# A two-layer hybrid mixer on one core: the convolution's taps held from before the stick heads until the choice of keys is done, their rest under the later early gates, and the convolution's norm behind the sparse heads

## The chip, the core and the metric

The kernel runs on one core of a Trainium2 chip. The metric is the device time of one execution in microseconds, as a median of several runs. The core has a matrix engine (TensorE, PE in the profile), a vector engine (DVE), a scalar engine (ACT), GpSimd (POOL), a queue engine that issues most transfers (SP) and 16 DMA engines. Each engine works through its own list of instructions in order; semaphores make one wait for another.

## What is computed

Two layers over 256 tokens of width 2048. Each layer normalises its input and projects it by one wide weight matrix; three token mixers work on the parts; their gated outputs are projected, merged by sigmoid gates, projected once more and added.

```python
h = rms_norm(x, norm_w)
proj = h @ w_in
(qa, ka, va, za, qi, ki, wi, ub, zb, qc, kc, vc, zc, gates) = jnp.split(proj, ...)
...
y_a = (dsa_attention(qa, ka, va, qi, ki, wi, top_k) * silu(za)) @ w_a_out
y_b = (conformer_conv(ub, conv_w, conv_b, cln_w, cln_b) * silu(zb)) @ w_b_out
y_c = (stick_breaking_attention(qc, kc, vc) * silu(zc)) @ w_c_out
g = sigmoid(gates).reshape(b, s, 3, D_MODEL)
merged = g[:, :, 0] * y_a + g[:, :, 1] * y_b + g[:, :, 2] * y_c
x = x + merged @ w_out
```

Branch A is a sparse attention: 16 small index heads (qi, ki, wi) score the keys, the 64 best of each query are chosen, and 8 heads attend to those alone. Branch B multiplies half of its projection by the sigmoid of the other, convolves each of 1024 channels over 31 past tokens, normalises over the channels and applies SiLU. Branch C is a stick-breaking attention of 8 heads: sigmoids of the products, running sums of logarithms over the keys, an exponential, and a product with the values.

## The kernel before

**Units and chunks.** All weights stream through PE in units of 512 KB. `load_unit` (L241) has SP issue the load into one of six `raw` buffers (L256); ACT rounds it to `wh` (`high`, L267), DVE subtracts to get the rest `wl` (`low`, L272); each has three buffers. PE multiplies both (all matmuls go through `mult`, L283). Eight units make a chunk of 512 columns (`chunk_W`, `chunk_N`); the chunk's sum stands in one of two `acc` tiles in PSUM, and a second pool of two tiles, `mm`, serves all smaller products. An `acc` tile is free again when its last reader is done, and the tile for a new chunk is given out by a scheduler that goes through the program as it will stand.

**Order of a layer.** After the convolution's input (`yT`) come, in this order on PE: the stick queries, keys and values (QC, KC, VC), the sparse queries QA (two chunks), index keys KI, values VA with the index weights, keys KA, index queries QI (eight chunks of 256), two early gates `early(1,0)` and `early(1,1)`, two more (`early(1,2)`, `early(1,3)`), then the branch gates ZC, ZB and ZA (two chunks each), the merging gates and the output projections.

**Work beside the units.** Three lists are advanced while the units run:
- `waiting` holds the convolution's taps. `taps` (L432) is four ACT activations (L441) and one DVE addition (L444) for four channel groups at one offset; 62 such taps per layer. `drain`, called by each `low`, runs at most one per unit, and none while `hold[0]` is set. `flush` runs all that is left at once.
- `turns` holds transpositions. `turn_in` (L171) copies an `acc` tile into two planes of 16 bits on ACT (L175), has SP issue two DMA transposes (L181) some units later, and joins the planes again (L189 on DVE, L191 on ACT or DVE).
- `stages` holds generators that yield after a number of units; `background` advances at most one turn or one of the first two stages per unit. `finish` runs them all to their end.

The generators that matter here: `stick` (L719) computes two stick heads: products, Abs/Exp/Ln on ACT, a split in two (L396, L397), the running sums as triangular products (L749 to L754), the difference (DVE L755), the exponential (ACT L756) and the mask (DVE L758), and the product with the values (L763, L765), copied by L767. `index_near` and `index_far` compute the index scores and choose the keys. `attend` (L907) computes four sparse heads for 128 queries: products (L915), softmax with exponentials on ACT (L924), transposes by DMA with ACT copies before and after (L933, L946), a split in two (L396, L397) and the product with the values (L953), copied by L955. `conv_norm` (L958) takes the means over channels by products with ones (L974), normalises, and applies SiLU. It needs all taps.

`early` (L898) multiplies one chunk of the merging gates ahead of its time, applies the sigmoid on ACT (L903, which needs another activation table than the copies) into a temporary of the pool `t4` (eight buffers, shared by taps, sticks and heads), and stores it by POOL (L904). `gate` (L408) multiplies a gate chunk, turns it with `turn_in` and applies SiLU.

**Where taps run before.** `hold[0]` goes up after QA's chunks (L786) and down after QI (L835). Before QA's end nearly all taps have run, one per unit; three entries are left for `flush()` (L957), which stands behind the first two early gates. `conv_norm` is started right there, then four `attend`, then `early(1,2)` and `early(1,3)`.

The instructions of each engine are written to a list by a scheduler that follows the order of the code, priorities (`high_priority`), `issue_after` and the buffers of the pools; so one moved call can move instructions of other calls.

Of the kernel before, what the change touches and what calls it, by code (L numbers as in the profile page):

```python
# [17 lines left out]
NT = S // P  # L18
# [38 lines left out]
def trunk(ctx: ExitStack, tc: tile.TileContext, x, xt, w_in, w_a, w_b, w_c, w_out,  # L57
# [38 lines left out]
    def nm(s):  # L96
        uid[0] += 1
        return f"{s}_{uid[0]}"
# [10 lines left out]
    def parts(n, own=()):  # L109
        own = list(own)  # L110
        return own + [slot(F32R).rearrange("p (k w) t -> p k w t", w=2) for _ in range(n // 4 - len(own))]
# [19 lines left out]
    def t4(dt=F32):  # L131
        return tp.tile([P, 1024], dt, tag="t4", bufs=8, name=nm("t4"))
# [7 lines left out]
    waiting = []  # L140
# [3 lines left out]
    def advance(e):  # L144
        try:
            e[1] = count[0] + next(e[0])
        except StopIteration:
            (stages if e in stages else turns).remove(e)
# [10 lines left out]
    def settle():  # L159
        while turns:  # L160
            advance(turns[0])
# [38 lines left out]
    def start(gen):  # L200
        stages.append([gen, 0])

    def finish():
        while stages:
            advance(stages[0])

    hold = [False]
# [12 lines left out]
    def flush():  # L220
        while waiting:
            for f in waiting.pop(0)[1]:
                f()
# [193 lines left out]
    def gate(c0, o, b, w, hx, park=None, slots=True, turn=TURN):  # L417
        def gated(k, z, v):
            nc.scalar.activation(v, z, AF.Silu)
            nc.vector.tensor_mul(z, v, o[:, k:k + 4, :])  # L420
            b.extend(parts(4))
            split_at(b, k, 4, z)
            if park is not None:
                for i in range(k, k + 4, 2):
                    nc.gpsimd.dma_start(park[:, i:i + 2], part(b, slice(0, 2), i, 2))

        for k in range(0, KC, 4):
            turn_in(chunk_W(w, c0 + k * P, hx), None, partial(gated, k), slots, turn)
# [60 lines left out]
    for layer in range(DEPTH):  # L489
# [277 lines left out]
            nc.scalar.copy(qcT[:, h0:h0 + 2, :], po[:, :512].rearrange("p (h t) -> p h t", h=2))  # L767

        settle()
        for h0 in range(0, NH, 2):  # L770
            start(stick(h0, STICK[h0 // 4]))

# [10 lines left out]

        for h in range(0, NH, 4):
            turn_in(chunk_W(w, O_QA + h * P, hx), qaT[:, h:h + 4, :], partial(spin, qaT[:, h:h + 4, :]))
        hold[0] = True  # L786
        kaT = t4()[:, :2 * S].rearrange("p (c t) -> p c t", c=2)
        ki = tp.tile([P, 2 * S], F32R, tag="ki", bufs=1, name=nm("ki")).rearrange("p (i c t) -> p i c t", i=2, c=1)
        rope(chunk_T(w, O_KI, P, hx, KD), None, partial(split, ki[:, 0], ki[:, 1]))
# [42 lines left out]
                turns.append([rotate(h - 2, v4), count[0]])  # L832
                advance(turns[-1])
        settle()
        hold[0] = False  # L835
        bias = {}

        def chosen(sc, bs, cb):
# [59 lines left out]
        def early(b, j):  # L898
            a = chunk_N(w, [(O_G + b * D + j * 512, 512)], hx, KD)
            sg_ = t4().rearrange("p (t d) -> p t d", t=NT)  # L900
            with tc.high_priority():
                for t in range(NT):
                    nc.scalar.activation(sg_[:, t, :], a[t], AF.Sigmoid)  # L903
            nc.gpsimd.dma_start(gates[b][:, :, j * 512:(j + 1) * 512].rearrange("t p d -> p t d"), sg_)  # L904
# [5 lines left out]
        def attend(t, c, qaT=qaT, kaT=kaT, va=va, bias=bias):  # L910
            n = (t + 1) * P
            ts_ = slice(t * P, (t + 1) * P)
            ps = mm_tile()
            for q in range(4):
                nc.tensor.matmul(ps[:, q * n:(q + 1) * n], qaT[:, c * 4 + q, ts_], kaT[:, c, :n],  # L915
                                 start=True, stop=True)
            lg = t4()
            l3 = lg[:, :4 * n].rearrange("p (h s) -> p h s", h=4)
            nc.vector.scalar_tensor_tensor(l3, ps[:, :4 * n].rearrange("p (h s) -> p h s", h=4), SCALE,
                                           heads(bias[t][:, :n], 4), op0=ALU.mult, op1=ALU.add)  # L920
            mx, sm = small(4), small(4)
            nc.vector.tensor_reduce(mx, l3, op=ALU.max, axis=AX.X, negate=True)
            for q in range(4):
                nc.scalar.activation(l3[:, q, :], l3[:, q, :], AF.Exp, bias=mx[:, q:q + 1],  # L924
                                     accum_out=sm[:, q:q + 1])
            nc.vector.reciprocal(sm, sm)
            nc.vector.tensor_mul(l3, l3, sm.unsqueeze(2).to_broadcast([P, 4, n]))
            own, cols = words(False)
            rows = own.rearrange("p (s w q k) -> p s w q k", s=NT, w=2, q=4)
            s16 = l3.bitcast(U16).rearrange("p q (s k w) -> p s q k w", k=P, w=2)  # L930
            for s in range(t + 1):
                for i in range(2):
                    nc.scalar.copy(rows[:, s, i], s16[:, s, :, :, i])  # L933
            yield 4
            for s in range(t + 1):
                    nc.sync.dma_start(cols.rearrange("p (g t) -> p g t", g=8)[:, :, s * P:(s + 1) * P],
                                      own[:, s * 1024:(s + 1) * 1024], transpose=True)
            yield 5
            c16 = cols.rearrange("p (w q s k) -> p w s q k", w=2, q=4, s=NT)
            into = own.bitcast(F32)[:, :4 * n]  # L940
            d16 = into.bitcast(U16).rearrange("p (s q k w) -> p s q k w", q=4, k=P, w=2)
            for s in range(t + 1):
                with tc.issue_after(lows[0].ins):
                    nc.vector.tensor_copy(d16[:, s, :, :, 1], c16[:, 1, s])
                with tc.issue_after(highs[0].ins):
                    nc.scalar.copy(d16[:, s, :, :, 0], c16[:, 0, s])  # L946
            ph, pl = pair(1024)
            split(ph[:, :4 * n], pl[:, :4 * n], into)
            yield 3
            po = mm_tile()  # L950
            for s in range(t + 1):
                for i, (u, v) in enumerate(((va[0], ph), (va[0], pl), (va[1], ph))):
                    nc.tensor.matmul(po[:, :512], u[:, s, c * P:(c + 1) * P], v[:, s * 512:(s + 1) * 512],  # L953
                                     start=s == 0 and i == 0, stop=s == t and i == 2)
            nc.scalar.copy(qaT[:, c * 4:c * 4 + 4, ts_], po[:, :512].rearrange("p (h t) -> p h t", h=4))  # L955

        flush()  # L957
        def conv_norm(cv=cv, pr=pr):  # L958
            work = t4()
            ph_ = pair(512)[0]  # L960

            def fold(w_, first, second):
                w4 = w_.rearrange("p (c t) -> p c t", c=4)
                nc.vector.tensor_add(w4, first, second)
                nc.vector.tensor_add(w_[:, :512], w_[:, :512], w_[:, 512:])
                nc.vector.tensor_add(w_[:, :S], w_[:, :S], w_[:, S:2 * S])
                h, l = ph_[:, :S], ph_[:, S:2 * S]
                nc.scalar.activation(h, w_[:, :S], AF.Copy, scale=1.0 / CW)
                nc.vector.scalar_tensor_tensor(l, w_[:, :S], 1.0 / CW, h.bitcast(F32), op0=ALU.mult, op1=ALU.subtract)

            def means():
                ps = mm_tile()
                for i in range(2):
                    nc.tensor.matmul(ps[:, :S], ones_r, ph_[:, i * S:(i + 1) * S], start=i == 0, stop=i == 1)  # L974
                return ps

            fold(work, cv[:, :4, :], cv[:, 4:, :])
            yield 3
            ps = means()
            sq = [t4().rearrange("p (c t) -> p c t", c=4) for _ in range(2)]  # L980
            for i in range(2):
                cs = cv[:, i * 4:i * 4 + 4, :]
                nc.vector.tensor_sub(cs, cs, heads(ps[:, :S], 4))
                nc.scalar.activation(sq[i], cs, AF.Square)
            fold(work, *sq)
            yield 6
            vs = means()
            r = rsqrt_mean(vs[:, :S], 1, t4())
            for i in range(2):
                cs = cv[:, i * 4:i * 4 + 4, :]  # L990
                nc.vector.tensor_mul(cs, cs, heads(r, 4))
                for c in range(4):
                    cc = i * 4 + c
                    lw, lb = pr[:, P_LW + cc:P_LW + cc + 1], pr[:, P_LB + cc:P_LB + cc + 1]
                    nc.scalar.activation(cs[:, c, :], cs[:, c, :], AF.Silu, bias=lb, scale=lw)
        start(conv_norm())
        for t in range(NT):
            for c in range(2):
                start(attend(t, c))


        for j in range(2, 4):
            early(1, j)
        gate(O_ZC, qcT, [], w, hx, parked[2], turn=OWN)
        gb = []
        gate(O_ZB, cv, gb, w, hx, slots=False, turn=LATE)
        finish()
        fast = FAST
        mix = [slot(F32R).rearrange("p a b -> p (a b)").rearrange("p (k i t) -> p k i t", k=KC, i=2)
# [304 lines left out]
```

## Time and profile before

| | us |
|---|---|
| median of 3 runs | 2026.02 (2025.62 to 2026.08) |
| the profiled execution | 2025.73 |
| its span, first to last instruction | 2024.0 |
| mean granted clock of PE | 0.997 of full speed |
| PE idle at L763, waiting for DVE L758 (2 times) | 4.1 |
| PE idle at L749, waiting for DVE L397 (2 times) | 1.8 |

The page of the profile gives busy time per engine and the groups of instructions. A row of the timeline has the start, the length, the engine, the line, the operation with its output and inputs, and, in brackets, how long the engine had been idle and who ended it. Consecutive instructions of one kind are one row with their number behind x. Where PE waits is also listed by line and cause. The granted clock is what the throttle left of full speed. Line numbers in the profile are those of the kernel before.

### The profile page before, as it was taken

What the parts mean: (1) busy time and instruction counts of PE and PEld (TensorE: products, weight loads), DVE (VectorE), ACT (ScalarE), POOL (GpSimd) and SP (SyncE); (2) the same over time, 40 slices, a digit from 0 to 9 for tenths busy, and PEclk for the clock granted to TensorE, in tenths of its full rate; (3) what the DMA queues carried; (4) which work ended last, traced back from release to release, by engine and by line L of the source; (5) the groups of instructions that cost most, each with busy time, mean ns of one, the idle gap of its engine ahead of it and who ended that gap; (6) DMA issues with size and microseconds to landing.
All of it is one profiled execution on the core that took longest, in us unless ns stands there. A gap on an engine that the chain in (4) does not pass through costs nothing. (4 is left out here: it accounts for less than half of the span.)

```text
span 2024.0 us, 26716 instructions
## 1 busy us (share of the span) xinstructions
PE 2006.2 (99%) x9566; PEld 1698.9 (84%) x9566; DVE 1560.7 (77%) x1708; ACT 1399.7 (69%) x1966; POOL 98.5 (5%) x156
## 2 busy tenths in 40 slices
PE   9999999999999999999999999999999999999998
PEld 7888889988888888888888888899888888888887
DVE  8688887797578888866676888878866888788665
ACT  7899696658776555556658997966587765555653
POOL 0000000000000100110000000000000012002100
PEclk9999999999999999999999999999999999999999
DMA  8788666766888877889867776666678999768983
GB/s 280 216 225 214 184 170 182 220 192 195 233 250 267 267 246 235 263 268 262 259 203 213 218 212 190 168 183 202 203 206 213 262 267 294 222 230 269 268 284 126
DMA packets 340278, 458.60 MB, mean 227 GB/s; under 512 B 109104, under 2 KB 159024, under 8 KB 340016
## 3 DMA queue, kind: packets, MB, share of 16 engines
q1 hardware_dynamic: 327040, 420.82, 71.2%
q0 software_dynamic: 11648, 33.56, 5.0%
q10 hardware_dynamic: 1456, 2.51, 0.4%
q8 instruction: 75, 1.23, 0.2%
q14 instruction: 59, 0.48, 0.1%
HBM read 413.30 MB, written 20.97 MB: 215 GB/s over the span
## 5 line engine op out<-in xcount | busy, mean ns | idle before, releaser
L283 PE MATMUL acc<-wh,s 128*128 128x512 f32 (+2 forms) x4736 | 1154.6, 386 | 1.5 <-ACT wh L267 1.5
L272 DVE TENSOR_TENSOR wl<-raw,wh 128x1024 fp32r<-128x1024 f32 (+1 forms) x714 | 858.6, 1207 | 316.1 <-ACT wh L267 312.3
L283 PEld LDWEIGHTS acc<-wh,s 128*128 128x128 f32 x4736 | 875.2, 188 | 178.7 <-ACT wh L267 2.8
L267 ACT CAST wh<-raw 128x1024 fp32r<-128x1024 f32 (+1 forms) x713 | 739.3, 1040 | 401.0 <-PE acc L283 323.7
L283 PE MATMUL acc<-wl,s 128*128 128x512 f32 (+2 forms) x2368 | 622.7, 385 | 0.2 <-DVE wl L272 0.2
L283 PEld LDWEIGHTS acc<-wl,s 128*128 128x128 f32 x2368 | 439.4, 188 | 89.7 <-DVE wl L272 0.6
L441 ACT ACTIVATE t<-s,cst 128x255 f32<-128x255 f32 (+14 forms) x480 | 199.1, 489 | 0.1
L444 DVE TENSOR_TENSOR s<-s,t 128x1020 f32<-128x1020 f32 (+14 forms) x120 | 138.6, 1155 | 1.5 <-ACT t L441 1.1
L283 PE MATMUL acc<-s,wh 128*128 128x384 f32 (+1 forms) x608 | 128.5, 353 | 0.0
L283 PE MATMUL mm<-wh,s 128*128 128x512 f32 x448 | 119.7, 389 | 0.0
L283 PEld LDWEIGHTS acc<-s,wh 128*128 128x128 f32 x608 | 106.3, 192 | 3.1
L283 PEld LDWEIGHTS mm<-wh,s 128*128 128x128 f32 x448 | 84.1, 188 | 17.5
L267 ACT CAST wh<-s 128x1024 fp32r<-128x1024 f32 x32 | 33.6, 1050 | 68.2 <-DVE s L1108 57.7
L283 PEld LDWEIGHTS acc<-s,wl 128*128 128x128 f32 x608 | 79.4, 191 | 1.0
L283 PE MATMUL acc<-s,wl 128*128 128x192 f32 (+1 forms) x608 | 79.8, 273 | 0.0
L234 POOL COPY sm<-sm 128x3 f32<-128x3 f32 x64 | 48.6, 759 | 502.1 <-ACT sm L233 502.1
L283 PE MATMUL mm<-wl,s 128*128 128x512 f32 x224 | 69.1, 390 | 0.0
L267 ACT CAST wh<-t 128x1024 fp32r<-128x1024 f32 x32 | 33.6, 1050 | 38.5 <-DVE t L1108 26.5
L904 POOL DMA_DIRECT2D gates<-t x8 | 6.0, 744 | 1108.1 <-ACT t L903 1058.9
L272 DVE TENSOR_TENSOR wl<-s,wh 128x1024 fp32r<-128x1024 f32 x32 | 39.2, 1225 | 26.0 <-ACT wh L267 25.8
L283 PEld LDWEIGHTS mm<-wl,s 128*128 128x128 f32 x224 | 41.9, 188 | 9.0 <-DVE wl L272 0.4
L272 DVE TENSOR_TENSOR wl<-t,wh 128x1024 fp32r<-128x1024 f32 x32 | 39.1, 1222 | 10.2 <-ACT wh L267 7.5
(241 smaller groups left out, 1277.1 us busy)
## 6 DMA issues: line engine op xcount, KB each, us to landing
raw<-in_w_in_dram SPq DMA_DIRECT2D x570, 512.0 KB, 4.4
raw<-in_w_out_dram SPq DMA_DIRECT2D x64, 512.0 KB, 5.3
raw<-in_w_b_dram SPq DMA_DIRECT2D x32, 512.0 KB, 5.0
raw<-in_w_c_dram SPq DMA_DIRECT2D x32, 512.0 KB, 4.9
raw<-in_w_a_dram SPq DMA_DIRECT2D x32, 512.0 KB, 5.5
parked<-s POOLq DMA_DIRECT2D x16, 512.0 KB, 5.8
t<-gates POOLq DMA_DIRECT2D x16, 512.0 KB, 6.5
s<-parked POOLq DMA_DIRECT2D x32, 256.0 KB, 5.6
```

Of the source, the lines that this page charges most:

```text
L234: seen = nc.gpsimd.tensor_copy(copy[:, :3], mark)
L267: highs[0] = nc.scalar.copy(u[1], u[0])
L272: sub = nc.vector.tensor_sub(u[2], u[0], u[1].bitcast(F32))
L283: newest[0] = nc.tensor.matmul(o, lhsT, rhs, start=start, stop=stop, skip_group_check=True)
L441: nc.scalar.activation(o[:, i, :S - d], yT[:, c, :S - d], AF.Copy, scale=wq)
L444: nc.vector.tensor_add(to, to, o[:, :, :S - d])
L904: nc.gpsimd.dma_start(gates[b][:, :, j * 512:(j + 1) * 512].rearrange("t p d -> p t d"), sg_)
```

## The change

`hold[0]` is set before the four stick generators are started, not after QA's chunks, and it is cleared after the first two early gates and the choice of keys (`finish()`), not after QI. The four `attend` are started before `early(1,2)` and `early(1,3)`, as these are written, and `conv_norm` behind both. `conv_norm` first yields, one unit at a time, until no tap is waiting. The call of `flush()` moves from ahead of it to behind the gates ZC and ZB.

In the order of the ACT engine, in layer 0, 17 taps move: 14 from units under QA and the sticks and 3 from the `flush`. They now stand one per unit in 17 units, from `early(1,2)` on into ZC.

The lines of the file shift: L903 becomes L902, L915 L914, L924 L923, L933 L932, L953 L952, L955 L954, L974 L982; those up to L767 move by one at most.

```diff
@@ -767,6 +767,7 @@
         settle()
+        hold[0] = True
         for h0 in range(0, NH, 2):
             start(stick(h0, STICK[h0 // 4]))
@@ -783,7 +784,6 @@
             turn_in(chunk_W(w, O_QA + h * P, hx), qaT[:, h:h + 4, :], partial(spin, qaT[:, h:h + 4, :]))
-        hold[0] = True
@@ -832,7 +832,6 @@
         settle()
-        hold[0] = False
         bias = {}
@@ -954,8 +953,17 @@
-        flush()
+        hold[0] = False
+        for t in range(NT):
+            for c in range(2):
+                start(attend(t, c))
+
+
+        for j in range(2, 4):
+            early(1, j)
         def conv_norm(cv=cv, pr=pr):
+            while waiting:
+                yield 1
             work = t4()
             ph_ = pair(512)[0]
@@ -994,16 +1002,10 @@
         start(conv_norm())
-        for t in range(NT):
-            for c in range(2):
-                start(attend(t, c))
-
-
-        for j in range(2, 4):
-            early(1, j)
         gate(O_ZC, qcT, [], w, hx, parked[2], turn=OWN)
         gb = []
         gate(O_ZB, cv, gb, w, hx, slots=False, turn=LATE)
+        flush()
         finish()
```

On PE, in the stretch of `early(1,3)` and the beginning of ZC, the value products of the heads stood between the units of ZC before (acc_772: ZC's first chunk, acc_801: its second):

```order
L283 MATMUL acc_772_4579<-wh_797_4715,s8_11_102 128x512 x8
L283 MATMUL acc_772_4579<-wl_798_4716,s8_11_102 128x512 x4
L953 MATMUL mm_799_4732<-ph_788_4674,t4_428_2534 128x512
L953 MATMUL mm_799_4732<-pl_789_4675,t4_428_2534 128x512
L953 MATMUL mm_799_4732<-ph_788_4674,t4_428_2534 128x512
L283 MATMUL acc_801_4740<-wh_803_4742,s8_8_99 128x512 x8
```

On PE after, the first of them stand inside the units (acc_719: `early(1,3)`, acc_770: ZC's first chunk):

```order
L283 MATMUL acc_719_4295<-wh_760_4503,s8_11_102 128x512 x6
L952 MATMUL mm_743_4422<-ph_728_4346,t4_414_2450 128x512
L283 MATMUL acc_719_4295<-wh_760_4503,s8_11_102 128x512 x2
L283 MATMUL acc_719_4295<-wl_761_4504,s8_11_102 128x512 x3
L952 MATMUL mm_748_4451<-ph_733_4370,t4_414_2450 128x512
```

The numbers in a name tell one tile from another. What moved: products of the heads' probabilities with the values now stand in the middle of a unit.

## The prediction

> **What bounds the kernel now.** I read the page's head first, then the waits of PE from 100 us on, then the timelines of PE, ACT, DVE and SP around each wait.
>
> ```profile
> span 2024.0 us, 26716 instructions
> PE 2006.2 (99%) x9566; PEld 1698.9 (84%) x9566; DVE 1560.7 (77%) x1708; ACT 1399.7 (69%) x1966; POOL 98.5 (5%) x156
> ```
>
> The profiled execution took 2025.73 us, 1.73 more than its span and 0.29 less than the median of 2026.02. PE, which multiplies the weight units, has work for 99% of the span. Time can be won only where PE stands still or runs at a lower clock, and anything that makes PE wait costs its full length. The waits of PE after the start are few:
>
> ```profile
> PE mm L763 <- DVE t L758: 4.1, 2, 2.1
> PE mm L749 <- DVE pl L397: 1.8, 2, 0.9
> PE acc L283 <- ACT wh L267: 0.4, 2, 0.3
> PE acc L283 <- DVE wl L272: 0.2, 1, 0.2
> ```
>
> The columns are total us, how often, and the longest one. Each of the first three comes once per layer, all at the stick heads (the generators `stick`, L719 to L767). In layer 0, on PE:
>
> ```profile
> 266.40 1.98 PE L283 MATMUL acc<-wh,s 128*128 128x512 f32 x8
> 269.12 1.98 PE L283 MATMUL acc<-wh,s 128*128 128x512 f32 x8
> ...
> 296.26 1.28 PE L283 MATMUL acc<-wh,s 128*128 128x272 f32 x8 [0.18 <-ACT wh L267]
> 297.38 0.66 PE L283 MATMUL acc<-wl,s 128*128 128x272 f32 x4
> 297.95 0.49 PE L749 MATMUL mm<-ph,upper_r 128*128 128x512 f32 x1
> 299.34 0.51 PE L749 MATMUL mm<-pl,upper_r 128*128 128x512 f32 x1 [0.90 <-DVE pl L397]
> ...
> 318.15 0.67 PE L763 MATMUL mm<-t,s 128*128 128x256 f32 x2 [2.03 <-DVE t L758]
> ```
>
> One full unit is 269.12 - 266.40 = 2.72 us of PE. The last unit of VA comes late by the cast (0.18 idle before it), then comes 0.90 behind L397, then 2.03 behind L758. And the last of these is followed by a lower granted clock. The columns of the windows are length, busy time of PE, PEld, DVE, ACT and POOL, granted clock, DMA share and GB/s:
>
> ```profile
> 299.00:304.00 5.00, 4.66 (x26) 4.10 (x27) 5.00 (x7) 4.94 (x7) 0.00 (x0) 1.00 0.95 302
> 318.00:323.00 5.00, 4.85 (x21) 4.65 (x22) 4.96 (x9) 2.89 (x6) 0.00 (x0) 0.66 0.37 108
> 323.00:330.00 7.00, 7.00 (x52) 7.00 (x51) 4.22 (x5) 3.65 (x5) 0.00 (x0) 1.00 0.48 128
> 1321.00:1326.00 5.00, 4.71 (x20) 4.58 (x21) 4.96 (x9) 2.96 (x6) 0.00 (x0) 0.66 0.37 108
> ```
>
> A clock of 0.66 over 5 us is (1 - 0.66) x 5 = 1.7 us of work not done, in both layers, each time behind the gap of two microseconds at L763. Behind the 0.90 at L749 there is none. So per layer the sticks cost about 0.2 + 0.9 at VA's end, and 2.0 + 1.7 at L763: 4.8 us, 9.6 in all. That is all that the first half of the change could win.
>
> **Part 1: the taps leave the sticks.** `hold` now goes up before the sticks start, so 17 taps per layer (14 in units under QA's chunks, 3 that `flush` put behind the gates) leave that stretch. What ACT does from the end of QA's last chunk on:
>
> ```profile
> 274.56 0.62 PE L283 MATMUL acc<-s,wh 128*128 128x512 f32 x2
> ```
> ```profile
> 274.81 1.91 ACT L175 COPY s<-acc 128x1024 uint16<-128x1024 uint16 x2
> 276.60 0.66 ACT L267 CAST wh<-raw 128x544 fp32r<-128x544 f32 x1
> 277.15 2.39 ACT L441 ACTIVATE t<-s,cst 128x230 f32<-128x230 f32 x6
> 279.43 0.58 ACT L767 COPY s<-mm 128x512 f32<-128x512 f32 x1
> 279.89 1.39 ACT L191 COPY s<-s 128x1024 uint16<-128x1024 uint16 x1
> 281.12 0.66 ACT L267 CAST wh<-raw 128x544 fp32r<-128x544 f32 x1
> 282.24 1.38 ACT L191 COPY s<-s 128x1024 uint16<-128x1024 uint16 x1 [0.46 <-DMA s<-s]
> ...
> 304.97 1.05 ACT L267 CAST wh<-raw 128x1024 fp32r<-128x1024 f32 x1 [0.98 <-PE acc L283]
> ```
> ```profile
> 276.74 3.41 SPq L181 DMA_TRANSPOSE s<-s  x2
> ```
>
> Taps run here as late as 277.15 to 279.43. But ACT then waits 0.46 for the transposes at 282.24, so it has caught up by then. Those transposes are issued by SP from 276.74, behind L175, whose start follows PE's end of the chunk at 274.56. None of this depends on the taps, so the second L191 starts at about 282.24 with them or without. After it ACT has no idle time until the 0.98 at 304.97, so the work up to VA's end is a chain from that L191 on. What the order changes there is one cast.
>
> On ACT, at the start of VA's units, before (wh_448 is the cast of a VA unit; the L191 rows are the two turns of QA's chunks):
>
> ```order
> L441 ACTIVATE t4_413_2441<-s8_80_536,cst_75 128x229 x4
> L767 COPY s8_137_854<-mm_421_2489 128x512
> L191 COPY s8_336_2021<-s8_379_2247 128x1024
> L267 CAST wh_448_2614<-raw_447_2613 128x544
> L191 COPY s8_336_2021<-s8_414_2461 128x1024
> L308 COPY ev_426_2523<-acc_417_2466 128x256
> ```
>
> On ACT, the same place after the change (wh_434 is that cast):
>
> ```order
> L191 COPY s8_336_2021<-s8_372_2205 128x1024
> L767 COPY s8_137_854<-mm_407_2405 128x512
> L191 COPY s8_336_2021<-s8_400_2377 128x1024
> L267 CAST wh_434_2530<-raw_433_2529 128x544
> L308 COPY ev_412_2439<-acc_403_2382 128x256
> ```
>
> The cast that filled ACT's wait for the transposes stands behind the second L191 now. It takes 277.15 - 276.60 = 0.55 us of ACT, and that much is added to the chain: +0.55 per layer at VA's end. The wait at L763 hangs on a chain that starts at KA's end, where ACT waits for PE once more:
>
> ```profile
> 312.56 0.59 ACT L308 COPY ev<-acc 128x512 f32<-128x512 f32 x1 [0.60 <-PE acc L283]
> ```
>
> So that wait stays, with its clock loss. Bounds for this part, per layer: -4.8 if all four losses go, -1.1 if only the two at VA's end go, +0.55 as worked out, and +0.55 + 1.7 if the gap at L749, then 1.45 us, starts a low-clock window too. I take +0.55, because the row at 282.24 shows a wait for DMA and not for taps.
>
> **Part 2: taps, attends and norm over the gates.** The 17 taps now run under `early(1,2)`, `early(1,3)` and the beginning of ZC. A tap is four activations:
>
> ```profile
> 261.97 1.05 ACT L267 CAST wh<-raw 128x1024 fp32r<-128x1024 f32 x1
> 262.93 1.63 ACT L441 ACTIVATE t<-s,cst 128x234 f32<-128x234 f32 x4
> 264.46 0.83 ACT L756 ACTIVATE t<-t 128x768 f32<-128x768 f32 x1
> ```
>
> A cast (0.96 to the next start) and a tap (1.53) are 2.49 of the 2.72 us of a unit, so the taps alone don't hold PE up; they leave ACT 0.23 us per unit for the heads' exponentials and copies, which have therefore moved later, onto ZC's units. Some products of `attend` (L915, L953; after: L914, L952) now stand inside units on PE, behind copies that ACT makes late. The order alone leaves them small margins. I take 0 for these, hidden by the three buffers of wh and wl; uncovered, one costs up to a late copy, about 1.05 us, at three such places per layer: 0 to +6.3 in all. Three taps leave `flush` and the norm moves behind the heads, towards ZB that uses it: 0, since the gates before it are 16 units or more long.
>
> **Part 3: the bank of ZC's second chunk.** A chunk accumulates in one of two `acc` tiles and frees it when ACT has copied it. The fourth early gate frees its tile with the sigmoids (L903, after: L902), ZC's first chunk with the pair at L175. On ACT before, at the end of ZC's first chunk (acc_729: the gate, acc_772: that chunk):
>
> ```order
> L903 ACTIVATE t4_771_4575<-acc_729_4356 128x512
> L267 CAST wh_797_4715<-raw_796_4714 128x1024
> L903 ACTIVATE t4_771_4575<-acc_729_4356 128x512
> L933 COPY t4_766_4550<-t4_763_4539 128x512 x2
> L267 CAST wh_803_4742<-raw_802_4741 128x1024
> L933 COPY t4_766_4550<-t4_763_4539 128x512
> L946 COPY t4_750_4471<-t4_751_4472 128x512
> L396 CAST ph_788_4674<-t4_750_4471 128x512
> L267 CAST wh_808_4768<-raw_807_4767 128x1024
> L946 COPY t4_766_4550<-t4_767_4551 128x512 x2
> L267 CAST wh_817_4808<-raw_816_4807 128x1024
> L175 COPY s8_800_4737<-acc_772_4579 128x2x512 x2
> ```
>
> On ACT after (acc_719: the gate, acc_770: ZC's first chunk):
>
> ```order
> L175 COPY s8_800_4727<-acc_770_4552 128x2x512 x2
> L932 COPY t4_767_4542<-t4_764_4531 128x512
> L902 ACT_TABLE_LOAD
> L902 ACTIVATE t4_769_4548<-acc_719_4295 128x512
> L267 CAST wh_815_4802<-raw_814_4801 128x1024
> L902 ACTIVATE t4_769_4548<-acc_719_4295 128x512
> ```
>
> On PE after, at the same boundary:
>
> ```order
> L283 MATMUL acc_770_4552<-wh_796_4702,s8_11_102 128x512 x8
> L283 MATMUL acc_770_4552<-wl_797_4703,s8_11_102 128x512 x4
> L283 MATMUL acc_801_4730<-wh_803_4732,s8_8_99 128x512 x8
> L283 MATMUL acc_801_4730<-wl_804_4733,s8_8_99 128x512 x4
> L283 MATMUL acc_801_4730<-wh_808_4758,s8_8_99 128x512 x8
> ```
>
> The sigmoids have moved from some ten rows ahead of the copies of ZC's first chunk to behind them: their t4 buffer comes free later, among the delayed taps and heads. So the tile that is free first for ZC's second chunk (acc_801) is that of ZC's first chunk itself: in the built program acc_801 lies in acc_770's banks (before, it alternated), and PE's first matmul of it waits for the second copy of L175, which can't start before PE has ended that very chunk. In the trace of before:
>
> ```profile
> 505.86 0.60 ACT L903 ACTIVATE t<-acc 128x512 f32<-128x512 f32 x1
> 507.29 0.60 ACT L903 ACTIVATE t<-acc 128x512 f32<-128x512 f32 x1
> ...
> 517.86 1.92 ACT L175 COPY s<-acc 128x1024 uint16<-128x1024 uint16 x2
> ```
>
> There the sigmoids end 10 us ahead of that boundary. The price: at QA's end the copies began 274.81 - 274.56 = 0.25 after PE's next start and took 1.91; a product starts about 0.05 behind its releaser, so PE stands for about 2.2 us, once per layer (bounds 1.9 to 2.5, by the start of L175 at the chunk's very end or behind a late cast). A gap of 2.03 was followed by 1.7 us of low clock in both layers, so I add that: 3.9 per layer. The Trainium skill ("TensorE: Matmul & The Clock Gate", section "What's actually happening") puts the half clock after at least one idle window of some 3.4 us; by it a gap of 2.2 us would cost only itself. The trace doesn't bear this out, since 2.03 us sufficed twice.
>
> **The sum.** 2025.73 + 2 x (0.55 + 2.2 + 1.7) = 2025.73 + 8.9 = 2034.6 as a profiled execution. With the 0.29 up to the median: 2034.9.
>
> **The rivals.**
> - *No low clock behind the new gap.* For it: the gap lies among full-clock units with a full supply of cast weights, and the gap of 0.90 had no such window. Against: 2.03 and its twin in layer 1. The Trainium skill's rule, above, is on this side. In both layers 2034.9 - 3.4 = 2031.5, in one 2033.2. Chance 0.17.
> - *More stalls*: the gap of 1.45 at L749 turns the clock down (+1.7 per layer), or the heads' products inside units wait for late copies (up to +3.1 per layer). For it: 0.23 us of ACT left per unit. Against: three buffers of slack. 2036.5 to 2041, chance 0.18.
> - *The sticks gain as well, beside the new gap.* Without taps all copies on ACT would start earlier than I think; this decides if the second L191 starts well ahead of 282.24. Against: that row waits for DMA. If the 1.1 at VA's end goes, 2034.9 - 2 x 1.65 = 2031.6; if all 4.8 go, the kernel is not slower: 2034.9 - 2 x (0.55 + 4.8) = 2024.2. Chance 0.04 each.
> - *Faster*: the sticks lose all their waits and PE finds acc_801's tile free. It needs L175 before the chunk's end, or another tile than the program shows: 2024.2 - 7.8 = 2016.4. Chance 0.03.
> - *Nothing reaches PE but the 0.55*: the bank wait is hidden, 2026.02 + 1.1 = 2027.1. Chance 0.04.
>
> **How the numbers follow.** The forecast itself has the remaining 0.50, with 2033.5 to 2036.5 as its own range by the bounds of the copies. 0.2% (4.05 us: 2021.97 and 2030.07) is about what a measurement of this kernel can tell from no change. Faster: 0.03. Same: 2024.2 and 2027.1, 0.04 + 0.04 = 0.08. Slower: the rest, 0.89. The range runs from 2031.0, just under the case without low clock, to 2040.0, which takes in most of the added stalls; outside lie the 0.11 of the three last cases and some 0.03 of the added stalls.
>
> **What would show it.** Right: in the waits of PE a new row, L283 behind ACT's L175, twice, about 2.2 each; a window of 0.66 or so behind it in each layer; L763 still 2.0 with its window; L749's wait 1.3 to 1.5 instead of 0.9; the sigmoids of the fourth early gate behind L175 in ACT's timeline. Wrong: no such wait, or no window behind it; L763's wait shorter; waits of PE at L914 or L952. If PE's busy time grows with no wait named, another cause lowered the clock.

## The result, and the profile after

The changed kernel takes 2040.49 us (median of 4 runs, 2038.46 to 2042.05), the kernel before 2026.05 (4 runs, 2025.62 to 2026.51): a ratio of 1.0071, with a 95% interval of 1.0053 to 1.0088. The direction was forecast, the size was not: 14.4 us instead of 8.9, half a microsecond above the range.

The profiled execution is the fastest of the four, at 2038.46 us, 12.7 more than the profiled one of before. The head of its page:

```profile
span 2036.7 us, 26721 instructions
PE 2009.9 (99%) x9566; PEld 1699.0 (83%) x9566; DVE 1561.5 (77%) x1708; ACT 1399.4 (69%) x1964; POOL 96.0 (5%) x156
```

DVE, ACT and PE's weight loads are as busy as before, within 1 us. PE is idle 9.0 us longer (26.8 instead of 17.8) and busy 3.7 us longer. The waits of PE from 100 us on (total us, times, longest):

```profile
PE acc L283 <- ACT s L175: 4.2, 2, 2.1
PE mm L763 <- DVE t L758: 4.1, 2, 2.1
PE mm L952 <- ACT ph L396: 3.0, 4, 1.1
PE acc L283 <- ACT wh L267: 1.8, 4, 0.7
PE mm L749 <- DVE pl L397: 1.8, 2, 0.9
PE acc L283 <- DVE wl L272: 1.5, 2, 1.0
```

The first row is the wait for the tile of ZC's second chunk, 2.1 once per layer; 2.2 was forecast. L763 and L749 stand as they stood; for L749 a wait of 1.3 to 1.5 was forecast, and it is 0.9. Against before there are two more new things: the heads' value products (L952) wait 3.0 in all, and the waits for casts at VA's end have grown from 0.4 to 1.8. On PE, around ZC's boundary and at the later heads:

```profile
515.09 1.07 PE L283 MATMUL acc<-wl,s 128*128 128x512 f32 x4
518.25 2.98 PE L283 MATMUL acc<-wh,s 128*128 128x512 f32 x8 [2.10 <-ACT s L175]
...
536.33 1.52 PE L283 MATMUL acc<-wh,s 128*128 128x512 f32 x6
538.27 0.51 PE L952 MATMUL mm<-ph,t 128*128 128x512 f32 x1 [0.41 <-ACT ph L396]
...
542.97 0.61 PE L283 MATMUL acc<-wl,s 128*128 128x512 f32 x2
544.66 0.50 PE L952 MATMUL mm<-ph,t 128*128 128x512 f32 x1 [1.08 <-ACT ph L396]
```

Four products of a wl take 0.91 (268.21 to 269.12 before, in the same kind of unit), so 518.25 - 515.09 - 0.91 = 2.25 us are lost at the boundary. At the heads, two wl products take 0.45: 544.66 - 542.97 - 0.45 = 1.24 lost; six wh products take 1.37: 538.27 - 536.33 - 1.37 = 0.57 lost. These waits come in the middle of a unit.

On ACT the copies that PE waits for at the boundary are

```profile
516.29 1.92 ACT L175 COPY s<-acc 128x1024 uint16<-128x1024 uint16 x2
```

and the sigmoids of the fourth early gate follow at 520.02 and 522.23, behind them, as forecast.

The chain of the third head group lost most of its time in SP's list, not on ACT. The copies and the first transposes of the third head group, in the changed kernel:

```profile
508.08 1.14 ACT L932 COPY t<-t 128x512 uint16<-128x512 uint16 x2
```
```profile
518.23 3.48 SPq L181 DMA_TRANSPOSE s<-s  x2
524.21 5.96 SPq L256 DMA_DIRECT2D raw<-in_w_in_dram  x3
530.26 3.33 SPq L935 DMA_TRANSPOSE t<-t  x2
```

The same in the run with the new order but early taps (below):

```profile
500.94 0.61 ACT L933 COPY t<-t 128x512 uint16<-128x512 uint16 x1
```
```profile
505.64 1.95 SPq L936 DMA_TRANSPOSE t<-t  x1
```

The copies end 7.7 us later (509.22 and 501.55), the first transpose is sent 24.6 us later. In the changed kernel it stands behind the transposes of ZC's first chunk (L181) and three more loads, and the profile shows no wait for data in front of it. So it is in all ten runs that have the new order: where the waits at the heads stay (the change in both its runs, sigmoids in ev, heads later, three repairs, ACT's half), the first transpose of this group goes out at 528 to 531, behind L181; where they go or shrink to 0.6 (taps left out, order alone, DVE's half, half the rate), at 505 to 513, ahead of it. Why the scheduler places it there isn't on record.

The windows of the clock, cut where the record of the granted clock changes (length, busy time of PE, PEld, DVE, ACT and POOL, granted clock, DMA share, GB/s). In the changed kernel, first around L763, then around ZC's boundary:

```profile
314.42:317.83 3.41, 2.65 (x19) 2.48 (x17) 3.38 (x6) 2.93 (x5) 0.00 (x0) 1.00 0.50 141
317.83:321.25 3.42, 2.12 (x13) 2.05 (x14) 3.08 (x6) 3.33 (x6) 0.00 (x0) 1.00 0.04 12
...
515.81:519.22 3.41, 1.31 (x6) 0.83 (x5) 1.95 (x2) 3.41 (x5) 0.00 (x0) 1.00 0.75 184
519.22:522.63 3.41, 3.41 (x9) 2.64 (x9) 0.00 (x0) 2.74 (x4) 0.00 (x0) 0.50 1.04 253
```

In the kernel before, around L763:

```profile
315.38:318.80 3.42, 1.39 (x11) 1.19 (x11) 3.04 (x6) 3.36 (x5) 0.00 (x0) 1.00 0.44 145
318.80:322.21 3.41, 3.41 (x14) 3.23 (x13) 3.41 (x6) 1.84 (x4) 0.00 (x0) 0.50 0.41 116
```

Half clock comes here for 3413 ns, after a stretch of the same length in which PE was busy for 1.3 or 1.4 us. The gap at L763 is as long after as before (2.06 and 2.03), but after, it falls across the edge of two stretches, which keep 2.65 and 2.12 us of work, and no half clock follows. The low-clock windows of this execution are therefore at ZC, as forecast, and no longer at L763, where the forecast had kept them.

The sum for the profiled execution, from start to start: ZC's boundary 2 x 2.25, the heads 2 x 1.8, VA's end about 1.3 in layer 0 (PE came to it 0.35 us earlier than before and left it 0.97 later) and 0.8 in layer 1 (below), one wait of 1.0 for L272 in the merging stage, and about 0.1 behind each of a dozen more switches between products and units. That is some 12 us. The low-clock windows are two in both executions and cancel.

The last unit of VA now starts with

```profile
297.23 1.27 PE L283 MATMUL acc<-wh,s 128*128 128x272 f32 x8 [0.66 <-ACT wh L267]
```

where it waited 0.18 at 296.26 before. Why that is 1 us later and not 0.55: on ACT after, at VA's start,

```profile
282.30 1.39 ACT L191 COPY s<-s 128x1024 uint16<-128x1024 uint16 x1 [3.22 <-DMA s<-s]
283.54 0.65 ACT L267 CAST wh<-raw 128x544 fp32r<-128x544 f32 x1
284.08 0.38 ACT L308 COPY ev<-acc 128x256 f32<-128x256 f32 x1
284.34 0.60 ACT L767 COPY s<-mm 128x512 f32<-128x512 f32 x1
285.31 0.40 ACT L408 COPY ev<-ev 64x256 f32<-64x256 f32 x1 [0.38 <-DVE ev L309]
```

and on DVE after:

```profile
284.22 0.73 DVE L272 TENSOR_TENSOR wl<-raw,wh 128x544 fp32r<-128x544 f32 x1 [1.13 <-ACT wh L267]
284.86 0.42 DVE L309 TENSOR_TENSOR ev<-acc,ev 128x256 f32<-128x256 f32 x1
```

ACT is idle for 3.22 us without the taps, and the second L191 still starts at 282.30, when the transposes land (282.24 before). The cast behind it costs its 0.55, and then its subtraction on DVE stands ahead of L309, for which ACT waits another 0.38.

### The profile page after: what moved, and what is told of

It reads as the page before. It is cut to its first block, busy times and chain, and to the rows that moved or that the text cites. A ratio compares the mean times of both kernels' runs of the same rounds, so it can differ in the third digit from the quotient of the medians.

```text
span 2036.7 us, 26721 instructions
## 1 busy us (share of the span) xinstructions
PE 2009.9 (99%) x9566; PEld 1699.0 (83%) x9566; DVE 1561.5 (77%) x1708; ACT 1399.4 (69%) x1964; POOL 96.0 (5%) x156
## 5 line engine op out<-in xcount | busy, mean ns | idle before, releaser
L272 DVE TENSOR_TENSOR wl<-raw,wh 128x1024 fp32r<-128x1024 f32 (+1 forms) x714 | 859.3, 1208 | 328.5 <-ACT wh L267 312.1
L903 POOL DMA_DIRECT2D gates<-t x8 | 6.0, 744 | 1137.7 <-ACT t L902 1137.7
L272 DVE TENSOR_TENSOR wl<-s,wh 128x1024 fp32r<-128x1024 f32 x32 | 39.2, 1225 | 26.0 <-ACT wh L267 25.8
L272 DVE TENSOR_TENSOR wl<-t,wh 128x1024 fp32r<-128x1024 f32 x32 | 39.1, 1223 | 9.9 <-ACT wh L267 7.1
## 6 DMA issues: line engine op xcount, KB each, us to landing
raw<-in_w_in_dram SPq DMA_DIRECT2D x570, 512.0 KB, 4.3
raw<-in_w_out_dram SPq DMA_DIRECT2D x64, 512.0 KB, 5.1
raw<-in_w_b_dram SPq DMA_DIRECT2D x32, 512.0 KB, 5.2
raw<-in_w_c_dram SPq DMA_DIRECT2D x32, 512.0 KB, 5.0
raw<-in_w_a_dram SPq DMA_DIRECT2D x32, 512.0 KB, 5.6
parked<-s POOLq DMA_DIRECT2D x16, 512.0 KB, 6.2
t<-gates POOLq DMA_DIRECT2D x16, 512.0 KB, 6.4
```

Source lines behind the costliest of these rows:

```text
L272: sub = nc.vector.tensor_sub(u[2], u[0], u[1].bitcast(F32))
```

## The experiments

All medians are of several runs. The kernel before ran on the same chip with each batch: 2025.69 in the first four experiments, 2025.45 in the next four, 2025.96 in the next three, 2025.75 in the last. The ratio is an estimate from all runs of both kernels, and so not exactly the quotient of the medians.

| run | median, us | ratio to before | 95% interval |
|---|---|---|---|
| the change again | 2039.55 | 1.0069 | 1.0054 to 1.0084 |
| sticks' half alone, taps left out | 2026.44 | 1.0005 | 0.9995 to 1.0014 |
| sigmoids in ev | 2037.46 | 1.0063 | 1.0045 to 1.0080 |
| the change, held taps left out | 2026.83 | 1.0008 | 0.9998 to 1.0017 |
| order alone | 2025.9 | 1.0000 | 0.9991 to 1.0009 |
| sigmoids in ev, heads later | 2032.43 | 1.0035 | 1.0021 to 1.0048 |
| before, sticks one unit later | 2021.13 | 0.9978 | 0.9969 to 0.9987 |
| the change with three repairs | 2029.2 | 1.0019 | 1.0010 to 1.0028 |
| before, sticks two units later | 2019.21 | 0.9967 | 0.9954 to 0.9979 |
| ACT's half of the held taps | 2042.83 | 1.0082 | 1.0068 to 1.0095 |
| DVE's half of the held taps | 2026.15 | 0.9999 | 0.9989 to 1.0008 |
| held taps at half the rate | 2033.97 | 1.0049 | 1.0031 to 1.0067 |

**The change again.** No edit.

> The changed kernel again, unaltered. Four runs of it lie between 2038.5 and 2042.1 us, and its profile has a half-clock window of 3413 ns behind each 2.1 us gap at ZC but none behind the gaps of 2.06 us at L763, which had them in the kernel before. Theory A: the granted clock is decided in windows of 3413 ns that run freely, so a gap of 2.1 us costs 1.7 us more only where most of it lies inside one window; then the time comes in steps of about 1.7 us between 2035 and 2042, and here the windows may stand behind other gaps than in the first profile, while the waits themselves are the same (4.2 at L175, 4.1 at L763, 3.0 at L952). Rival B: a gap at L763 no longer lowers the clock because the work around it has changed; then the two windows are at ZC again.

2039.55 us (2038.71 to 2040.88). Its profile has the same waits (4.2 at L175, 4.1 at L763, 2.5 at L952), and three windows of half clock: behind both gaps at ZC, and behind L763 in layer 1 but not in layer 0, where the gap of 2.06 again falls across an edge (0.73 and 1.33). One and the same wait costs 1.7 us more or doesn't, in one and the same program. (The other waits of this execution are 1.7 us shorter in all, so its time is that of the first profile within 0.3.) Theory A holds, B falls.

**The sticks' half alone.** The kernel before, with

```diff
         settle()
+        hold[0] = True
         for h0 in range(0, NH, 2):
...
-        hold[0] = True
...
         hold[0] = False
+        waiting.clear()
```

> The kernel before with the hold from before the sticks on, and the 17 taps per layer that are then left are left out altogether; all else as before. What the first half of the change does by itself. Theory A (as predicted, with the size seen after): the sticks gain nothing; VA's units end about 1.0 us later per layer because one cast stands behind the second L191; the wait at L763 stays 2.0: 2026.05 + 2.0 = 2028.1, or down to 2024.6 if the windows of low clock miss the gaps. Rival: the taps held up the sticks' chain, and the waits at L749 and L763 shrink: 2016 to 2024.

2026.44 us. In its profile the waits at L763 and L749 are as before (4.1 and 1.8), and those for casts 1.6. Without a single tap in their stretch the sticks gain nothing: the rival falls. The median is 1.7 below what A expected and within the spread of half-clock windows (its profile has none behind L763).

**Taps or order.** In the changed kernel the held taps are left out altogether:

```diff
         hold[0] = False
+        waiting.clear()
         for t in range(NT):
```

> The changed kernel with the 17 taps per layer left out that would run under the later early gates; the order of attends, gates and norm as in the changed kernel. Tells whether the taps or the new order of the heads make the waits. Theory A: the taps make them: no wait for L175, none at L952 (its products stand between units again); what is left is VA's 1.0 per layer: 2028.1, less up to 3.5 if low clock misses L763's gaps. Rival: the heads started ahead of the early gates cost by themselves; then about 3.9 per two layers of the waits at L952 stay: 2032.

2026.83 us. Its waits of PE:

```profile
PE mm L763 <- DVE t L758: 4.1, 2, 2.1
PE acc L283 <- DVE wl L272: 2.2, 2, 1.8
PE acc L283 <- ACT wh L267: 1.8, 4, 0.7
PE mm L749 <- DVE pl L397: 1.8, 2, 0.9
```

No wait at L175, none at L952. The taps make both; the new order of heads, gates and norm doesn't. The 1.8 at L272 lies in the merging stage of layer 1, where DVE waits for a transfer; it differs from execution to execution.

The other way round, the new order with the taps where they were. The kernel before, with the hold and the first `flush` as they stand there, and

```diff
         flush()
+        for t in range(NT):
+            for c in range(2):
+                start(attend(t, c))
...
+        for j in range(2, 4):
+            early(1, j)
         def conv_norm(cv=cv, pr=pr):
+            while waiting:
+                yield 1
...
         start(conv_norm())
-        for t in range(NT):
-            for c in range(2):
-                start(attend(t, c))
...
-        for j in range(2, 4):
-            early(1, j)
...
+        flush()
         finish()
```

> The second half of the change alone: taps as in the kernel before (hold after QA's chunks, the last three by flush behind the first two early gates), but the heads started ahead of early(1,2) and early(1,3) and the norm behind them. Its products stand between units, and the early sigmoids ahead of ZC's copies. Theory A (the taps on ACT make the waits, not the order): as the kernel before, 2025.7, within 1.5. Rival: the order itself delays the heads' transposes, and waits of 1 us or more at L952 appear: 2028 to 2030.

2025.9 us, a ratio of 1.0000. The order by itself costs nothing and brings nothing. No run has the late taps under the old order of heads, gates and norm, so whether the taps would make the waits there too stays open.

**Which half of a tap.** In the changed kernel the held taps do only their activations, or only their additions:

```diff
-        o = cv[:, c0:c0 + 4, :] if last else t4().rearrange("p (c t) -> p c t", c=4)
+        o = cv[:, c0:c0 + 4, :] if last else yT[:, c0:c0 + 4, :] if late[0] else t4().rearrange("p (c t) -> p c t", c=4)
...
-            else:
+            elif not late[0]:
                 nc.scalar.activation(o[:, i, :S - d], yT[:, c, :S - d], AF.Copy, scale=wq)
```
```diff
-        if not last:
+        if not last and not late[0]:
             to = cv[:, c0:c0 + 4, d:]
```

(the first is DVE's half alone, the second ACT's half alone; `late` is set where the hold goes up.)

> The changed kernel in which the 17 taps per layer under the gates do only their four activations on ACT; their additions on DVE are left out. Theory A (ACT's time makes the heads late): products of the heads still stand inside units and wait for L396 on ACT, 3 us per layer now that no bank wait hides part of it (on ACT the early sigmoids stand ahead of ZC's copies, since a tap's t4 buffer is free as soon as ACT is done): 2032 to 2037. Rival (DVE's additions make them late): the waits go, 2027.

> The changed kernel in which the 17 taps per layer under the gates do only their additions on DVE, with the unscaled input; the activations on ACT are left out, and no t4 buffer is used. Theory A (ACT): no waits at L175 and L952, 2026.8 as without the taps at all. Rival (DVE): waits of 1 us or more at the heads' products, 2030 or more.

DVE's half alone: 2026.15 us, and no new wait but VA's. ACT's half alone: 2042.83 us, more than the whole change. Its largest waits of PE (its lines stand one lower):

```profile
PE mm L953 <- ACT ph L397: 6.3, 6, 2.0
PE acc L284 <- ACT t L903: 5.6, 2, 2.8
PE mm L764 <- DVE t L759: 4.1, 2, 2.1
```

It is ACT's half of a tap that makes the heads and the sigmoids late. DVE's half alone also takes no t4 buffer, so the time of the activations and the buffers that they fill are not told apart. The size was missed, since I had expected the bank wait to go with the order of the sigmoids: acc tiles now alternate, but the sigmoids end so late that PE waits for them instead, 2.8 per layer. Which tile is given out decided only who is waited for.

**The bank wait by itself.** The sigmoids of the changed kernel are written to `ev`, not to `t4`:

```diff
-            sg_ = t4().rearrange("p (t d) -> p t d", t=NT)
+            sg_ = [ev() for _ in range(NT)]
...
```

> The changed kernel with the sigmoids of the early gates written to two ev tiles, not to a t4 tile, so that they needn't wait for a t4 buffer; on ACT they then stand ahead of the copies of ZC's first chunk. Theory A: the wait of 2.1 per layer for L175 goes, with its window of low clock: 2040.5 - 2 x (2.1 + 1.7) = 2032.9; if windows then stand behind L763's gaps, up to 2036. The waits at L952 (3.0 in all) stay or change little. Rival: the second chunk's tile is not bound to the sigmoids, the wait stays and the time is 2040.

2037.46 us. The wait at L175 is gone, so the t4 buffer was its cause, but the time has hardly followed:

```profile
PE mm L953 <- ACT ph L396: 6.2, 2, 3.1
PE mm L763 <- DVE t L758: 4.1, 2, 2.1
```

On ACT, ahead of the product that waits 3.11 (at 540.49):

```profile
535.47 0.78 ACT L946 COPY t<-t 128x512 uint16<-128x512 uint16 x1 [1.73 <-DMA t<-t]
537.82 0.76 ACT L946 COPY t<-t 128x512 uint16<-128x512 uint16 x1 [1.57 <-DMA t<-t]
538.45 1.03 ACT L267 CAST wh<-raw 128x1024 fp32r<-128x1024 f32 x1
539.39 1.04 ACT L396 CAST ph<-t 128x1024 fp32r<-128x1024 f32 x1
```

The third head group's transposes were sent as late as in the changed kernel (529.78, there 530.26), though its copies had ended at 512.0, and its chain ends when it ends. In the changed kernel PE had stood 2.1 at ZC's boundary ahead of it, and so waited only 0.4 and 1.1 here. Two waits in a row hide each other; taking away the first pays little. The low clock didn't go either: half clock follows the gap of 3.1 in both layers, in layer 1 for two stretches in a row.

**Repairs of the change.** In addition, the heads' value products three units later (`yield 6` for `yield 3` ahead of `po`):

> The changed kernel with the sigmoids in ev tiles (as in the run with 2037.5 us, whose bank wait went and whose wait at L953 became 3.1 us per layer) and the heads' value products three units later (the last yield of attend 6, not 3). Theory A: the heads' chain on ACT and DMA ends late by a fixed time and PE needs only other work till then; the waits of 3.1 and their windows of low clock go: 2037.5 - 2 x (3.1 + 1.7) = 2027.9, about what the sticks' half gives alone (2026.4). Rival: the products, norm and ZB are then late themselves, and a new wait comes behind: 2031 or more.

2032.43 us; the rival is right. The one wait of 3.1 per layer has become several small ones: L953 3.6 in seven waits, and 1.2 once at L915. Its profile also shows the edge of the clock rule. The stretch that holds most of L763's gap (1.79 us of it):

```profile
317.10:320.51 3.41, 1.62 (x10) 1.55 (x11) 3.04 (x6) 3.34 (x6) 0.00 (x0) 1.00 0.15 53
320.51:323.92 3.41, 3.41 (x24) 3.41 (x23) 3.38 (x7) 1.95 (x3) 0.00 (x0) 1.00 0.52 159
```

and, in the kernel with the taps left out, a stretch with a gap of 1.81:

```profile
1653.19:1656.60 3.41, 1.60 (x7) 1.00 (x6) 3.22 (x3) 0.79 (x1) 0.91 (x2) 1.00 0.88 306
1656.60:1660.01 3.41, 3.41 (x9) 2.65 (x8) 2.54 (x3) 0.26 (x1) 0.00 (x0) 0.50 0.81 258
```

With the sticks' products one unit later too (the edit of the next paragraph):

> The changed kernel with all three repairs: sigmoids in ev tiles, the heads' value products three units later, the last two stick pairs' products one unit later. Theory A: each wait is repaired at its own place, and what stays of the change is the cast of VA behind the second L191, 1.0 to 1.5 per layer: 2017.8 + 2 to 3 = 2020 to 2021, slower than the kernel before with its sticks repaired. Rival (the idea of the change): with the taps gone and the waits repaired the sticks' stretch runs without loss, 2016 to 2018.

2029.2 us. Both expectations are missed. The sticks' waits shrank as they do without the change, but the heads' products still wait 4.3 in all in the profiled execution, which was the slowest of eleven (2032.66). The repairs do not bring the change down to the kernel before.

**The sticks by themselves.** In the kernel before the last two pairs' products are moved:

```diff
-STICK = ((10, 5), (7, 4))
+STICK = ((10, 5), (8, 4))
...
-        finish()
         qa2 = slot(F32R)...
...
             total(chunk_T(w, O_QI + h * P, 256, hx, KD, TOPK), v4[:, h % 4:h % 4 + 2, :])
+            if h == 0:
+                with tc.issue_after(newest[0].ins):
+                    finish()
+                qa2 = slot(F32R)...
```

> The kernel before, not the changed one, with the last two stick pairs' products placed one unit later on PE: the third pair waits 8 units, not 7, before its sums, and the last finish stands behind QI's first chunk, not ahead of it. Theory A: the waits at L749 (0.9) and L763 (2.05 with low clock behind it in about 6 of 10) come from PE reaching them too early, and one unit of 2.4 to 2.8 us covers both: 2025.7 - 2 x (0.9 + 2.05 + 1.0) = 2017.8. Rival: the chain that ends at L758 is held by ACT and DVE work of the same units, so it moves later with PE, and the gain is under 2 us.

2021.13 us, a ratio of 0.9978 (0.9969 to 0.9987). The waits at L763 fall from 4.1 to 1.7, those at L749 from 1.8 to 1.4, and no gap over 0.9 us is left there, so no half clock follows. The products came about one unit later, but each wait at L763 shrank by only 1.2: the chain moved along with PE by the rest, so a part of the gain is lost. A's 2017.8 is too low, and the rival, right that the chain moves, is refuted in its "under 2 us". With STICK at (9, 5):

> The kernel before with the last two stick pairs later still: the third pair waits 9 units before its sums, and 5 more before its values, so that both value products stand behind QI's first chunk. One unit later left waits of 1.7 at L763, 1.4 at L749 and 1.0 for casts and gave 2021.1. Theory A (PE reaches the sticks too early): the rest of the waits at L749 and L763 goes too, 2021.1 - 3.1 = 2018. Rival: ACT and DVE are full in these units, and their casts come late now in place of the sticks' waits: 2020 to 2022.

2019.21 us, 0.9967 (0.9954 to 0.9979): faster than both kernels.

```profile
PE acc L283 <- DVE wl L272: 1.4, 2, 0.8
PE mm L749 <- ACT ph L396: 1.3, 2, 0.6
PE acc L283 <- ACT wh L267: 0.4, 1, 0.4
```

No wait at L763 is left. What the change wanted from fewer taps came from asking one or two units later.

**Taps at half the rate.** The changed kernel, with

```diff
         hold[0] = False
+        for n, it in enumerate(waiting):
+            it[0] = 2 * n
```

> The changed kernel with the 17 held taps spread out, one in every second unit, not in every one; nothing else. Theory A (ACT has 0.23 us per unit left with a tap in each, and the heads' copies and sigmoids queue up): with 1.0 us per unit left the early sigmoids stand ahead of ZC's copies again, the wait for L175 goes, and those at L952 shrink below 1 us per layer: 2026 to 2029, as with the taps left out (2026.8). Rival: the sum of ACT work up to the heads' end counts, not its rate, or ZB now waits for the norm, which starts 16 units later: 2031 or more.

2033.97 us. Its waits of PE besides L763 (4.1) and L749 (1.8):

```profile
PE acc L283 <- DVE wl L272: 3.7, 2, 2.7
PE acc L283 <- ACT wh L267: 1.5, 3, 0.7
PE mm L952 <- ACT ph L396: 0.6, 2, 0.4
```

The waits at L175 and L952 behave as A says: gone, and 0.6. The rate isn't all that changed, though: in the trace no tap runs between 485.4 and 512.3, where the third head group's exponentials and copies are made, while in the changed kernel 21 activations stand there. And the median is 2034.0, not under 2029: two waits of 1.0 and 2.7 at L272 in the merging stages, where DVE waits for a transfer of POOL's queue, appear in this profile. Whether the norm's later place makes them or they vary by themselves stays open; it wasn't tried.

## Why the prediction was wrong in size

- **Part 3, the bank wait: right.** It was forecast from the order on ACT and PE and priced at 2.2 from two rows of QA's end; measured 2.10 idle, 2.25 from start to start, in both layers. That the late t4 buffer causes it was shown by the run with ev tiles.
- **Part 1, no gain at the sticks: right**, shown by leaving the taps out. The row on which it rested (ACT waiting 0.46 for the transposes) became a wait of 3.22 with the start of L191 unmoved. The 0.55 was undersized: 1.3 and 0.8, and the delay didn't lengthen the wait at L749 to 1.45, it came as waits for casts of VA (0.29 and 0.66 in layer 0). The step missed that a cast brings a subtraction with it, on another engine, ahead of what ACT needs next.
- **Part 2, "I take 0 for these, hidden by the three buffers of wh and wl": this step failed.** The three buffers hold casts ahead; they don't hold the heads' chain ahead. The products inside units waited 1.5 per layer, 1.8 from start to start, twice over: 3.6 us. The 0.23 us is the margin of a unit with one tap; in the trace the 17 taps of layer 0 stand unevenly, with up to eight activations between two casts and none in ten other units. Against the run with the order alone the third group's copies are 7.7 us late, and SP's list, which the prediction didn't look at for the heads, makes the transposes 24.6 us late. A chain of so many pieces over three engines' lists should have got the value of the bound's middle, 3 us, not 0. This is the largest term that was missing; the switches between products and units added some 1.2. By the prediction's own signs ("waits of PE at L914 or L952") this shows it wrong; its rival "more stalls" (2036.5 to 2041, chance 0.18) came true, by the heads and not by L749.
- **The clock: half right.** A gap of 2.1 us was followed by half clock at ZC in all four cases of the two profiles of the change. (In the first of them the gaps of the two layers end at 518.25 and 1528.28, which is 295.9 stretches apart, so both fall on nearly the same place of a stretch and are hardly two trials.) But "1.7 for each gap of about 2 us" was wrong as a rule: it depends on where the gap lies in a grid of 3413 ns, so the windows at L763 of the kernel before weren't a fixed cost either. With the bound found below (1.8 of 3.41), a gap of 2.1 lies enough within one stretch at (3.41 + 2.1 - 2 x 1.8) / 3.41 = 0.56 of all places, if every place is as likely: an estimate of 1.0 us, not 1.7, for each gap. In the profiled execution the 3.4 us of this term came to nothing, since L763's two windows were gone; it is luck that this hid most of the 4.8 us of heads and switches there (12.7 measured, 8.9 forecast).
- **The median** stood 2 us above the profiled execution, the fastest of its four; the forecast had allowed 0.3. Four such gaps, each with or without its 1.7 us, would spread the runs like that (2038.46 to 2042.05); it wasn't traced run by run.

## What to carry to other kernels

Work that is moved off a stretch helps only if the stretch waits for that engine: here one row (an engine waiting for a transfer, not for its own queue) told that it didn't. Where work is moved to, ask what reserve the engine has left per unit and which chains run through it at that time; a reserve of a tenth is none for a chain of many steps. Where such a chain passes through the list of a queue engine, look at what it then stands behind: here transposes whose copies had ended at 509 were sent at 530. And where PE meets a product too early, moving the product one or two units later is the cheaper cure.

## What the runs showed of the hardware

Half clock comes in stretches of 3413 ns on a grid that runs through the whole execution: in the kernel before, the two begin at 318.80 and 1322.31 us, 1003.51 apart, 294 times 3.4133. A stretch followed when one gap of 1.81 us or more lay within a single stretch of the grid (1.81, 2.03 to 2.06, 2.10 and longer, 16 cases in nine profiles), and none behind a full-clock stretch when the largest part was 1.79 or less (1.79, 1.65, 1.56, 1.51, 1.47 and shorter). So the bound lies near half of the stretch. Once, in the run with the sigmoids in ev, a stretch at half clock with only 0.67 us idle, the rest of the gap that had begun before it, was followed by a second one. In all these cases the idle time of the stretch is one gap; whether several short ones add up the same way is not shown. The kernel before, with two gaps of 2.0, ran between 2023.47 and 2028.34 us in 27 runs of one batch; the kernel with the sticks two units later, without a gap over 0.9, between 2018.53 and 2019.63 in 5.

The Trainium skill ("TensorE: Matmul & The Clock Gate", section "What's actually happening") describes a free-running window of 3413 ns, which these records show as well. It says that the clock falls after at least one idle window; here it fell after windows in which PE was busy for 0.3 to 1.6 us.
